# GELU times a gate, streamed through one core: the first tile stored in pieces of two and six rows, the last tile computed in its own input buffer

## The chip, the cores and the metric

The kernel runs on one core of a Trainium2 chip. The metric is the device time of one execution in microseconds (us), the median of several runs. ScalarE (ACT in the profile) computes the GELU, VectorE (DVE) the product, and SyncE (SP) and ScalarE issue DMA transfers. Each of the two issuing engines has a DMA queue of its own; both queues are served by the same 16 DMA engines. TensorE does nothing here.

## The reference

The input x has the shape (32, 512, 2048) in float32. Each row of 2048 is cut into two halves, and the output is the GELU of the first half times the second half:

```
half_dim = x.shape[-1] // 2
x1, x2 = (x[..., :half_dim].copy(), x[..., half_dim:].copy())
gelu_x1 = 0.5 * x1 * (1 + erf(x1 / np.sqrt(2)))
return (gelu_x1 * x2).astype(np.float32)
```

That is 134.2 MB read and 67.1 MB written, and three operations or so for each output element.

## The kernel before

The 16384 rows are cut into 16 tiles of 1024 rows. In a tile every one of the 128 partitions holds R = 8 consecutive rows, so a load of a tile is 8.39 MB, 64 KB in one piece for each partition, and a store is 4.19 MB, 32 KB in one piece for each partition. There are two input buffers (`x_bufs`, each 8 x 2048 floats per partition) and two output buffers (`o_bufs`, each 8 x 1024 floats). Tile i uses the buffers k = i % 2.

The program writes its order and its semaphores by hand. What counts is the order on each engine's own stream:

- SyncE issues the loads (`load`, L48 to L51). Before the loop it issues tile 0 in two halves (rows 0-3 and rows 4-7, here called loads 0a and 0b) and then load 1. In the loop, after tile i's products, it waits for all of them (L114) and issues load i+2 into the buffer that tile i has just given up (L115). At the end it also issues the stores of the last two tiles: store 14 (L110) and the two halves of tile 15, here called stores 15a and 15b (L105).
- ScalarE computes the GELU in steps of rows (L86 to L92): rows 0-1, 2-3 and 4-7 for the first and the last tile, rows 0-4 and 5-7 for the others. It writes the GELU into the output buffer. It also issues the stores of tiles 0 to 13 (L107 and L112), each after waiting for the products it stores (`store`, L53 to L57). Since ScalarE works its stream in order, it can't begin the next GELU while it waits to issue a store. Tile 0 is stored in two halves: rows 0-3 (store 0a) after the products of rows 2-3, and rows 4-7 (store 0b) after the last.
- VectorE multiplies each step in the output buffer by the second halves of the rows (L93 to L102), after waiting for that step's GELU.

Before a tile's first GELU ScalarE waits on one semaphore for its buffer, `ready[k]` (L85; tile 0 waits on `first` instead, L83). Load i counts on it, and so does the store of tile i-2, which has to be out of the output buffer before it is written again. Thus tile i waits for both, and tile 15 for load 15 and store 13. Stores 14, 15a and 15b count on another semaphore, `tail_stored`, which SyncE waits for at the very end (L125).

Of the kernel before, what the change touches and what calls it, by code (L numbers as in the profile page):

```python
# [1 line left out]

# [4 lines left out]

GELU = mybir.ActivationFunctionType.Gelu


@with_exitstack
def kernel(
    ctx: ExitStack,
    tc: tile.TileContext,
    x: bass.AP,
    out: bass.AP,
):
    nc = tc.nc
    P = nc.NUM_PARTITIONS

    x_flat = x.flatten_outer_dims()
    out_flat = out.flatten_outer_dims()
    n_rows, dim = x_flat.shape
    half = dim // 2

    R = 8
    x_t = x_flat.rearrange("(n p r) d -> n p r d", p=P, r=R)
    o_t = out_flat.rearrange("(n p r) d -> n p r d", p=P, r=R)
    n_tiles = x_t.shape[0]
    x_bufs = [nc.alloc_sbuf_tensor(f"x{k}_tile", [P, R, dim], x.dtype) for k in range(2)]  # L30
    o_bufs = [nc.alloc_sbuf_tensor(f"o{k}_tile", [P, R, half], out.dtype) for k in range(2)]

    first = [nc.alloc_semaphore(f"first{j}") for j in range(2)]
    ready = [nc.alloc_semaphore(f"ready{k}") for k in range(2)]
    gelu_done = nc.alloc_semaphore("gelu_done")
    mul_done = nc.alloc_semaphore("mul_done")
    tail_stored = nc.alloc_semaphore("tail_stored")
    opened = nc.alloc_semaphore("opened")  # L40
    scrap = nc.alloc_sbuf_tensor("scrap_tile", [8, 128], x.dtype)
    n = {sem.name: 0 for sem in [*first, *ready, gelu_done, mul_done, tail_stored, opened]}

    def counted(ins, sem, by):
        ins.then_inc(sem, by)
        n[sem.name] += by

    def load(i, rows, sem):  # L48
        ins = nc.sync.dma_start(out=x_bufs[i % 2][:, rows, :], in_=x_t[i][:, rows, :])  # L49
        counted(ins, sem, 16)  # L50
        return ins  # L51

    def store(queue, i, rows, sem):  # L53
        queue.wait_ge(mul_done, n[mul_done.name])
        counted(
            queue.dma_start(out=o_t[i][:, rows, :], in_=o_bufs[i % 2][:, rows, :]), sem, 16
        )  # L57

    opening = nc.scalar.dma_start(out=scrap[:, :], in_=x_t[0][:8, 0, :128])
    counted(opening, opened, 16)
    for ins in (
        opening,
        load(0, slice(0, 4), first[0]),
        load(0, slice(4, 8), first[1]),
        load(1, slice(0, 8), ready[1]),
    ):  # L70
        tc.no_tile_sem_insts.add(ins.ins.name)
    tc.close()
    tc.compile()  # L73

    for i in range(n_tiles):
        k = i % 2
        last = i == n_tiles - 1
        pieces = i == 0 or last
        steps = ((0, 2), (2, 4), (4, 8)) if pieces else ((0, 5), (5, 8))
        for lo, hi in steps:  # L80
            rows = slice(lo, hi)
            if i == 0 and lo % 4 == 0:
                nc.scalar.wait_ge(first[lo // 4], 16)  # L83
            elif lo == 0:
                nc.scalar.wait_ge(ready[k], n[ready[k].name])  # L85
            counted(  # L86
                nc.scalar.activation(  # L87
                    out=o_bufs[k][:, rows, :], in_=x_bufs[k][:, rows, :half], func=GELU
                ),
                gelu_done,  # L90
                1,
            )  # L92
            nc.vector.wait_ge(gelu_done, n[gelu_done.name])  # L93
            counted(
                nc.vector.tensor_mul(  # L95
                    out=o_bufs[k][:, rows, :],
                    in0=o_bufs[k][:, rows, :],
                    in1=x_bufs[k][:, rows, half:],
                ),
                mul_done,  # L100
                1,
            )  # L102
            if pieces and hi % 4 == 0:
                if last:
                    store(nc.sync, i, slice(hi - 4, hi), tail_stored)  # L105
                else:
                    store(nc.scalar, i, slice(hi - 4, hi), ready[k])  # L107
        if not pieces:
            if i == n_tiles - 2:
                store(nc.sync, i, slice(0, R), tail_stored)  # L110
            else:
                store(nc.scalar, i, slice(0, R), ready[k])  # L112
        if i + 2 < n_tiles:
            nc.sync.wait_ge(mul_done, n[mul_done.name])  # L114
            load(i + 2, slice(0, R), ready[k])  # L115


    nc.scalar.wait_ge(opened, 16)
    nc.scalar.drain()  # L119
    for sem in (*first, *ready, opened):  # L120
        nc.scalar.sem_clear(sem)
    nc.vector.drain()
    nc.vector.sem_clear(gelu_done)
    nc.sync.sem_clear(mul_done)
    nc.sync.wait_ge(tail_stored, n[tail_stored.name]).then_inc(  # L125
        tail_stored, -n[tail_stored.name]
    )


# [1 line left out]
_INS = ['x']  # L131
_OUTS = [((32, 512, 1024), 'float32')]


# [23 lines left out]
```

## Time and profile before

| what | value |
|---|---|
| device time, median of 3 runs | 469.3 us (469.29 to 469.43) |
| profiled execution: span from the first to the last instruction (the page gives no other time of it) | 467.8 us |
| VectorE busy | 140.5 us, 34 products |
| ScalarE busy | 115.5 us, 34 GELUs and one table load |
| DMA | 201.34 MB, 430 GB/s in the mean |
| one tile of 8 rows in the steady stretch | 29.0 us |
| median from issue to landing: whole load, whole store by ScalarE | 44.4 us, 44.7 us |

The span is cut into 40 slices in the page, and a row of digits gives the busy tenths of each engine in each slice; the DMA row is the mean over the 16 DMA engines. The chain of waits goes back from the last instruction through whatever released each step. A wait for several things at once is put down to the one that came last. The trace also has a record of every DMA packet with its queue, size, start and duration, and of every semaphore update.

### The profile page before, as it was taken

The numbers are of one execution on the slowest core, as the hardware profiler recorded it, in microseconds if no ns is written. First come the engines' busy times: TensorE is split into PE (matmuls) and PEld (weight loads), VectorE is DVE, ScalarE is ACT, GpSimd is POOL, SyncE is SP. The second block draws the span as 40 slices with busy tenths as digits, with TensorE's granted clock in tenths as the row PEclk, the third lists the DMA queues.
The fourth block names the chain that finished last, engine by engine and source line by source line (L and its number), as shares of the span: only waits on it lengthen the run. The fifth ranks groups of instructions, "written<-read, shape, count | busy, mean of one in ns | idle before, by whom it ended". The sixth has DMA issues, their size and how long they took to land.

```text
span 467.8 us, 154 instructions
## 1 busy us (share of the span) xinstructions
DVE 140.5 (30%) x34; ACT 115.5 (25%) x35; POOL 0.2 (0%) x4
## 2 busy tenths in 40 slices
DVE  0330515207051060511606115060150702507043
ACT  1320606041060410604105050050501506014060
POOL 0000000000000000000000000000000000000000
DMA  8999999999999999999999999999999999999988
GB/s 359 448 448 448 398 406 496 403 403 448 459 437 403 440 412 493 403 403 448 487 409 403 445 406 493 403 403 448 493 403 403 448 426 471 403 426 426 493 384 379
DMA packets 5057, 201.34 MB, mean 430 GB/s; under 512 B 568, under 2 KB 576, under 8 KB 576
## 3 DMA queue, kind: packets, MB, share of 16 engines
q1 hardware_dynamic: 2880, 142.61, 70.6%
q10 hardware_dynamic: 2176, 58.73, 29.1%
q14 instruction: 1, 0.01, 0.0%
HBM read 134.22 MB, written 67.11 MB: 430 GB/s over the span
## 4 chain that ended last, share of the span: by engine, by line
DMA 76%; DVE 14%; ACT 8%; ACTq 0%; SPq 0%; issue 0%
DMA out_dram<-o_tile 66%; DVE o_tile L95 14%; DMA x_tile<-in_x_dram 10%; ACT o_tile L87 8%; ACTq L119 0%; SPq L49 0%
## 5 line engine op out<-in xcount | busy, mean ns | idle before, releaser
L95 DVE TENSOR_TENSOR o_tile<-o_tile,x_tile 128x5120 f32<-128x5120 f32 (+3 forms) x34 | 140.5, 4171 | 319.7 <-ACT o_tile L87 319.7
L87 ACT ACTIVATE o_tile<-x_tile 128x5120 f32<-128x5120 f32 (+3 forms) x34 | 114.3, 3407 | 337.3 <-DMA out_dram<-o_tile 301.8
L87 ACT ACT_TABLE_LOAD x1 | 1.3, 1283 | 2.9 <-PEq L73 2.9
L142 POOL MEMSET const-bfloat16-1.0<- 128x1 bf16 x1 | 0.1, 102 | 0.0
L142 POOL MEMSET const-uint8-127<- 128x1 uint8 x1 | 0.1, 101 | 0.0
L142 POOL MEMSET const-float32-0.0<- 128x1 f32 x1 | 0.1, 99 | 0.2 <-issue 0.2
L142 POOL MEMSET const-float32-1.0<- 128x1 f32 x1 | 0.1, 98 | 0.0
## 6 DMA issues: line engine op xcount, KB each, us to landing
out_dram<-o_tile ACTq DMA_DIRECT2D x13, 4096.0 KB, 44.7
x_tile<-in_x_dram SPq DMA_DIRECT2D x2, 4096.0 KB, 16.7
out_dram<-o_tile ACTq DMA_DIRECT2D x2, 2048.0 KB, 34.4
out_dram<-o_tile SPq DMA_DIRECT2D x1, 4096.0 KB, 25.2
out_dram<-o_tile SPq DMA_DIRECT2D x2, 2048.0 KB, 7.8
x_tile<-in_x_dram SPq DMA_DIRECT2D x15, 44.4
scrap_tile<-in_x_dram ACTq DMA_DIRECT2D x1, 4.0 KB
```

The source lines that it names most:

```text
L87: nc.scalar.activation(out=o_bufs[k][:, rows, :], in_=x_bufs[k][:, rows, :half], func=GELU),
L95: nc.vector.tensor_mul(out=o_bufs[k][:, rows, :], in0=o_bufs[k][:, rows, :], in1=x_bufs[k][:, rows, half:],),
L142: nc = _bacc.Bacc("TRN2", target_bir_lowering=False, num_devices=1)
```

## The change

Two things change. First, tile 0 is stored as rows 0-1 (2048 floats, 8 KB per partition, 1.05 MB in all) and rows 2-7 (24 KB per partition, 3.15 MB). The store of rows 0-1 stands at the same place in ScalarE's stream as store 0a did, after the GELU of rows 2-3, but waits only for the product of rows 0-1. The store of rows 2-7 stands where store 0b did and waits for all products of the tile.

Second, tile 15 no longer uses an output buffer. Its GELU is written over the first halves of its rows in the input buffer, and the product is written packed into the front of the same buffer: the product of rows r takes the place of 1024 floats from 1024 r on, which lies over input that has been used by then. VectorE therefore also waits for its own earlier product before each product of this tile. Stores 15a and 15b read from the packed place. Tile 15 needs nothing of output buffer 1, so store 13 counts on `tail_stored` instead of `ready[1]`, and tile 15 waits for load 15 alone.

The number of instructions on each engine, the number of DMA transfers, and the order of all other steps stay as they were.

```diff
-    def store(queue, i, rows, sem):
-        queue.wait_ge(mul_done, n[mul_done.name])
-        counted(
-            queue.dma_start(out=o_t[i][:, rows, :], in_=o_bufs[i % 2][:, rows, :]), sem, 16
-        )
+    def store(queue, i, rows, from_, sem, after):
+        queue.wait_ge(mul_done, after)
+        counted(queue.dma_start(out=o_t[i][:, rows, :], in_=from_[:, rows, :]), sem, 16)
...
+    packed = x_bufs[(n_tiles - 1) % 2][:, :, :].rearrange("p r d -> p (r d)")
+    packed = packed[:, : R * half].rearrange("p (r d) -> p r d", d=half)
     for i in range(n_tiles):
         k = i % 2
+        x_buf = x_bufs[k]
         last = i == n_tiles - 1
+        made = packed if last else o_bufs[k][:, :, :]
...
+            gelu = x_buf[:, rows, :half] if last else made[:, rows, :]
             counted(
-                nc.scalar.activation(
-                    out=o_bufs[k][:, rows, :], in_=x_bufs[k][:, rows, :half], func=GELU
-                ),
+                nc.scalar.activation(out=gelu, in_=x_buf[:, rows, :half], func=GELU),
                 gelu_done,
                 1,
             )
+            if last:
+                nc.vector.wait_ge(mul_done, n[mul_done.name])
             nc.vector.wait_ge(gelu_done, n[gelu_done.name])
             counted(
                 nc.vector.tensor_mul(
-                    out=o_bufs[k][:, rows, :],
-                    in0=o_bufs[k][:, rows, :],
-                    in1=x_bufs[k][:, rows, half:],
+                    out=made[:, rows, :], in0=gelu, in1=x_buf[:, rows, half:]
                 ),
                 mul_done,
                 1,
             )
-            if pieces and hi % 4 == 0:
-                if last:
-                    store(nc.sync, i, slice(hi - 4, hi), tail_stored)
-                else:
-                    store(nc.scalar, i, slice(hi - 4, hi), ready[k])
+            done = n[mul_done.name]
+            if last and hi % 4 == 0:
+                store(nc.sync, i, slice(hi - 4, hi), made, tail_stored, done)
+            elif i == 0 and hi == 4:
+                store(nc.scalar, i, slice(0, 2), made, ready[k], done - 1)
+            elif i == 0 and hi == 8:
+                store(nc.scalar, i, slice(2, 8), made, ready[k], done)
         if not pieces:
-            if i == n_tiles - 2:
-                store(nc.sync, i, slice(0, R), tail_stored)
-            else:
-                store(nc.scalar, i, slice(0, R), ready[k])
+            queue = nc.sync if i == n_tiles - 2 else nc.scalar
+            sem = ready[k] if i < n_tiles - 3 else tail_stored
+            store(queue, i, slice(0, R), made, sem, done)
```

## The prediction

> **What bounds the kernel now.** I read the slices of the page first, to see whether anything has idle time; then the groups by shape and the chain of waits, to see what the engines wait for; then the DMA issues and the DMA records of the trace, to see in what order the transfers go; and last the order of instructions at both ends, where a change of stores can act.
>
> The page, its span, its slices and its bytes:
>
> ```profile
> span 467.8 us, 154 instructions
> ...
> DVE  0330515207051060511606115060150702507043
> ACT  1320606041060410604105050050501506014060
> ...
> DMA  8999999999999999999999999999999999999988
> ...
> HBM read 134.22 MB, written 67.11 MB: 430 GB/s over the span
> ```
>
> ScalarE and VectorE idle two thirds of the time; the DMA engines are at nine tenths or more in every slice but the first and the last two, and those are where both parts of the change act. So the question is how much of these edges is really idle. Stretches of the span (columns: length, busy time of each engine, granted clock, DMA share, rate):
>
> ```profile
> 71.40:100.40 29.00, 8.76 (x2) 7.12 (x2) 0.00 (x0) 1.00 1.00 434
> 100.40:448.50 348.10, 105.13 (x24) 85.47 (x24) 0.00 (x0) 1.00 1.00 432
> 448.50:457.60 9.10, 6.34 (x3) 7.21 (x3) 0.00 (x0) 1.00 1.00 432
> 457.60:467.40 9.80, 2.58 (x1) 0.00 (x0) 0.00 (x0) 1.00 0.94 402
> 467.40:467.80 0.40, 0.00 (x0) 0.00 (x0) 0.00 (x0) 1.00 0.00 0
> ```
>
> One tile (8.39 MB in, 4.19 MB out) takes 29.0 us at 434 GB/s, and the tail goes at that rate until the last half microsecond. The DMA records say it more sharply: a 64 KB packet takes 2.418 us, a 32 KB one 1.213, a 16 KB one 0.611 (and one 8 KB packet of the instruction queue 0.309), whether read or written. Each of the 16 DMA engines has 120 packets of 64 KB, 128 of 32 KB and 32 of 16 KB: 290.2 + 155.3 + 19.6 = 465.0 us. The first packet starts at 1.74 and the last ends at 467.37, which is 465.6 us. What is not plain moving is 0.6 us of slow first packets at 1.7 to 4, and about 0.4 us of packets that run over their usual time between 21 and 47 (neighbouring packets overlap a little, so the terms exceed the whole by 0.4). Gaps between packets are under 0.1 us each. The kernel is as long as its bytes.
>
> The chain of waits (start, length, what), its end:
>
> ```profile
> 403.75 44.74 DMA out_dram<-o_tile
> 448.49 0.02 issue
> 448.51 1.91 ACT o_tile L87
> 450.42 1.80 ACTq L119
> 452.22 3.52 ACT o_tile L87
> 455.73 0.02 issue
> 455.76 4.42 DVE o_tile L95
> ```
>
> This seems to name the change's target: the last tile (15) begins when store 13 lands, 44.74 us after its issue. But the issues of the x tile, and the waits, say what is beside it:
>
> ```profile
> DMA to landing us min/median/max: 12.0/44.4/45.4
> ...
> ACT o_tile L87 <- DMA out_dram<-o_tile: 301.8, 14, 21.9
> ACT o_tile L87 <- DMA x_tile<-in_x_dram: 35.6, 3, 20.9
> ```
>
> Load 15, issued at 403.74, takes 44.4, so it lands at about 448.1. In the DMA records the two queues take turns packet by packet (a 64 KB load packet, then a 32 KB store packet), 8 packets of each on every engine, so store 13 and load 15 end within one packet, and the 32 semaphore updates of both arrive between 447.88 and 448.49. The wait on the store is 0.1 to 0.4 us longer than that on the load.
>
> **Part 1, the last tile in its own buffer.** Removed: tile 15's wait for store 13, at most 448.49 - 447.88 = 0.6, by the medians 0.35 us. Is it on the path that sets the end? SyncE issues stores 14, 15a and 15b:
>
> ```profile
> 432.76 27.78 SPq L56 DMA_DIRECT2D out_dram<-o_tile  x3
> 448.51 7.21 ACT L87 ACTIVATE o_tile<-x_tile 128x2048 f32<-128x2048 f32 x3 [21.91 <-DMA out_dram<-o_tile]
> 450.45 4.49 DVE L95 TENSOR_TENSOR o_tile<-o_tile,x_tile 128x2048 f32<-128x2048 f32 x2 [17.71 <-ACT o_tile L87]
> 455.76 4.42 DVE L95 TENSOR_TENSOR o_tile<-o_tile,x_tile 128x4096 f32<-128x4096 f32 x1 [0.81 <-ACT o_tile L87]
> ```
>
> Store 14 was issued at 432.76 but stands behind load 15 on the same queue. By the DMA records its packets run from 447.51 to 457.2-457.6, store 15a from there to 462.06-462.5, and store 15b to 466.9-467.4, with no gap. Store 15a is issued at 455.0, some 2.2 us before the engines need it; 15b at 460.2, 1.85 us before. A first load at the start needs 1.0 us from issue (0.73) to its first packet (1.74), so tile 15 has about 1.2 and 0.85 us to spare. An earlier start only lengthens these. Worth: 0.
>
> Added: two VectorE waits on VectorE's own earlier products. The two products of 2048 that now run in 4.49 us are 2.288 each, so they overlap by 0.09; with the wait the second loses this and about 0.02 for the release (the "issue" rows of the chain): 0.1 us on store 15a, which has 1.2 to spare. The second wait, before the product of 4096, is already satisfied (products of rows 2-3 end at 454.94, it starts at 455.76). Nothing but stores 15a and 15b waits for VectorE there. For this wait VectorE: DVE Perf Modes (The DRAIN you can't avoid) of the Trainium skill says that chained copies with a semaphore after each took as long as without; by it this 0.1 would be 0, and as the sum takes it as hidden, the time is the same by both.
>
> Changed: the GELU writes 2x1024 and 4x1024 with a stride inside the x tile, and the product writes packed into the x tile with both inputs strided. No row of before shows a strided output. Before, one input of the product and the GELU's input were strided already. From below the cost is nothing (the element count is the same, a gain is excluded since no work is left out). From above I take the fixed part doubled: by the rows 2048 -> 2.288 and 4096 -> 4.424 VectorE has 0.15 us fixed; by 1.901 and 3.608 ScalarE has 0.19; along GELU, GELU, GELU, product to store 15b that is 0.73 us, still under 0.85. I take 0, since the strided input shows no price; without the cover it would be +0.73. The stores of tile 15 read 16 KB in one piece per partition as before.
>
> **Part 2, tile 0.** Its product of rows 0-1 ends at 14.73 + 2.29 = 17.02, and ScalarE is free at 12.79 + 3.71 = 16.50, so store 0a goes out at 17.04 instead of 19.26, with 8 KB packets; rows 2-3 wait for rows 4-7 and go in 24 KB packets. Moved bytes are equal, and the packets of one pair take 0.309 + about 0.912 (halfway between 16 and 32 KB) = 1.22 against 2 x 0.611 = 1.22 us: 0. ScalarE is not held longer: its wait is shorter by 2.2 us and the GELU of rows 4-7 waits for load 0b anyway.
>
> Next: load 0b runs until 22.1. Before, store 0a's first packet ran at 24.4, after load 1's first. Two microseconds earlier it gets one or two turns before load 0b's end, 0.31 us each: rows 4-7 land 0.3 to 0.6 us later, and so do store 0b and load 2 (issued at 30.5 and 30.6, now about 31). Load 1 fills the DMA until 45 or more, so both are covered by 14 us; without that cover they would cost the 0.6. Then stores run n = 1 or 2 packets ahead of where they ran: load 1 shares its time with 8 packets of 0.31 and n of 0.91 instead of 8 of 0.61, so it lands at 47.0 - 2.4 + 0.9n = 45.5 (n = 1) or 46.4. Load 2 then takes in n packets of store 1 and lands 1.2n later than 71.4, and so do all later ones; store i-2 lands before load i. In every later period store i is issued 13.3 us after load i lands (tile 1: 47.02 to 60.31), long before store i-1 runs out, and even without a store the load alone fills the engines: load 0b alone moved 4.19 MB in 9.7 us, 433 GB/s. Before tile 15 all bytes of loads and of stores to 13 have gone by, so load 15's last packet still ends at 447.5. Worth: 0.
>
> Unknown: the 0.4 us of stretched packets at 21 to 47, of which 0.25 lies in load 1's first packet, where the store queue joins. It could vanish (-0.4) or double with the earlier joining (+0.4). I take it unchanged, since a joining stays.
>
> **Sum.** 467.8 + 0 + 0 = 467.8 of span. The page gives no time of the profiled execution but its span; the median of the timed runs, 469.3, is 1.5 us above it, and what lies around the span (launch, clearing of semaphores) is not touched. Forecast: 469.3.
>
> **The rivals.**
>
> Slower, at the tail: the in-place forms cost more than my bound, so store 15b comes late and the DMA engines run dry at 462. It decides from 0.85 us more on the way from the start of tile 15 to the issue of 15b, and shows as slower from 1.8. If the product of 4096 took twice its 4.42: +4.4 - 0.85 = +3.6, 472.9. For it: no strided output in the trace. Against: strided inputs already run at 1.04 ns per element. Chance 0.04.
>
> Slower, at the start: each 8 KB store packet stretches the load packet beside it as load 1's first was (0.25): 8 x 0.25 = 2.0, less the 0.25 paid today: 471.1. Against: 16 KB packets did so once of eight. Chance 0.03.
>
> Faster: the chain is right, and the end follows the start of tile 15. By the landings this gives 0.35, 469.0, and only from 0.94 would it show; store 13 would have to land that much after load 15. Against: store 14 fills the DMA until 457.2 anyway. Chance 0.02 for over 0.94.
>
> The memory, not the DMA engines, sets the rate, so the new order of reads and writes changes it. Rows: reads alone 433, mixed 434, writes alone 432 GB/s. If mixing cost as much as the 430 to 434 difference of whole span and steady stretch, 0.9%, over one tile's 29 us, it is 0.3 us either way: 469.0 to 469.6. Chance 0.03 that it goes beyond 0.94, shared 0.01 and 0.02. DMA: Bandwidth & Descriptors (Where 436 GB/s comes from) of the Trainium skill says that for HBM transfers the HBM limit of about 358 GB/s binds; by it, as an estimate, 201.3 MB would take 562 us, and the trace with 430 GB/s does not agree.
>
> **How the numbers follow.** Timed runs of before lie within 0.14 us, but I take 0.2% (0.94 us) as what this kernel can tell from no change. Forecast 0.88, the rivals 0.04, 0.03, 0.02 and 0.03. Slower: 0.04 + 0.03 + 0.02 = 0.09; faster: 0.02 + 0.01 = 0.03; same 0.88. The range takes the stretched packets both ways (469.3 - 0.4 and + 0.4) and 0.1 more above for a tail that uses up its cover: 468.9 to 469.8.
>
> **What would show it.** Store 0a issued near 17.0; tile 1 starting at about 45.5 instead of 47.02; the tiles after it starting 1 to 2.5 us later than before; most of ScalarE's 301.8 us of waiting put down to loads instead of stores; tile 15 starting at 448.1 to 448.5; the last three stores landing without a gap at about 457.9, 462.9 and 467.8. I am wrong if the DMA share drops below 0.9 between 457 and 467, if load packets beside 8 KB packets grow, or if a stretch in the middle falls under 434.

## The result and the profile after

The changed kernel takes 469.86 us (median of 21 runs, 469.59 to 470.25), the kernel before 469.31 (median of 21). The ratio is 1.0012 with a 95% interval of 1.0006 to 1.0017: 0.55 us slower. The forecast was 469.3, with a range that ended at 469.8.

The page of the changed kernel, its span, its slices and its bytes:

```profile
span 468.6 us, 157 instructions
...
DVE  0330512407034070330704307042070520705143
ACT  1330606014060230602306032060320604106060
...
DMA  8999999999999999999999999999999999999998
...
HBM read 134.22 MB, written 67.11 MB: 430 GB/s over the span
```

The span is 0.8 us longer (468.62 against 467.84), the bytes are the same, and the DMA engines are still busy in every slice. The three instructions more (154 before) are VectorE's waits on its own products. Stretches of the changed kernel (columns as before: length, busy time of each engine, granted clock, DMA share, rate):

```profile
71.40:100.40 29.00, 8.76 (x2) 7.12 (x2) 0.00 (x0) 1.00 1.00 434
103.40:451.00 347.60, 105.19 (x25) 87.52 (x26) 0.00 (x0) 1.00 1.00 434
```

So nothing was lost in the steady stretch: 29.0 us for a tile's bytes at 434 GB/s, as before. The end, in order of time:

```profile
435.67 0.35 SPq L55 DMA_DIRECT2D out_dram<-o_tile  x1
448.91 7.22 ACT L90 ACTIVATE x_tile<-x_tile 128x2048 f32<-128x2048 f32 x3 [19.41 <-DMA x_tile<-in_x_dram]
450.93 4.62 DVE L98 TENSOR_TENSOR x_tile<-x_tile 128x2048 f32<-128x2048 f32 x2 [15.29 <-ACT x_tile L90]
455.58 5.44 SPq L55 DMA_DIRECT2D out_dram<-x_tile  x2
456.23 4.42 DVE L98 TENSOR_TENSOR x_tile<-x_tile 128x4096 f32<-128x4096 f32 x1 [0.68 <-ACT x_tile L90]
```

Tile 15 now waits for its load alone, and still starts 0.4 us later than before (448.91 against 448.51). Its GELUs take 7.22 us (7.21 before) and the last product the same 4.42. The tail did what it did before, some tenths later. And the beginning:

```profile
17.03 0.38 ACTq L55 DMA_DIRECT2D out_dram<-o_tile  x1
23.66 3.62 ACT L90 ACTIVATE o_tile<-x_tile 128x4096 f32<-128x4096 f32 x1 [7.18 <-DMA x_tile<-in_x_dram]
27.31 4.43 DVE L98 TENSOR_TENSOR o_tile<-o_tile,x_tile 128x4096 f32<-128x4096 f32 x1 [8.10 <-ACT o_tile L90]
31.76 0.36 ACTq L55 DMA_DIRECT2D out_dram<-o_tile  x1
47.13 7.12 ACT L90 ACTIVATE o_tile<-x_tile 128x5120 f32<-128x5120 f32 x2 [19.86 <-DMA x_tile<-in_x_dram]
```

Store 0a goes out at 17.03, 2.2 us earlier, as the change says. But the second half of tile 0 lands 1.2 us later (its GELU starts at 23.66, not 22.47), and tile 1 starts at 47.13 where 45.5 to 46.4 was forecast.

The records of the DMA packets show the loss itself. A record doesn't name its DMA engine, but each packet starts within a few ns of the end of another, and followed in this way the records fall into 16 chains, one for each engine. Below are the packets of one chain in both kernels: start in us, L for a load and S for a store, size in KB, and after a plus the ns over the usual time of that size (8 KB 309, 16 KB 611, 24 KB 912, 32 KB 1213, 64 KB 2418).

```
before: 20.5:L32 21.7:L64+381 24.5:S16 25.1:L64 27.5:S16 28.1:L64 30.5:S16 ... 43.3:L64 45.7:S16 46.3:L64 48.7:S16
after:  18.2:L32 19.4:L32+552 21.2:S8 21.5:L32 22.7:S8 23.0:S8 23.3:L64 25.8:S8 ... 36.6:S8 36.9:L64 39.4:L64+69 41.8:S24 42.8:L64+164 45.3:S24
```

The load packet that is under way when a store begins takes longer. Before, this happens once, when store 0a joins load 1. After, it happens twice: when store 0a joins load 0b, and again around store 0b's first 24 KB packet, in load 1's last two packets. (This is the order in 12 of the 16 chains. In the other four one more load packet goes ahead of the store's first packet both times; the first time the stretched packet is the one ahead of that load packet, the second time it is that load packet itself.) Summed over all packets that took longer than usual between 10 and 70 us and divided by 16 engines, it is 0.41 us before and 1.03 after. The difference, 0.62, accounts for the 0.55 us of the medians and for most of the 0.78 by which the last packet ends later (468.15 against 467.37); in the mean over the 16 chains the last packet ends 0.64 later. After 70 us the sum is 0.03 in either kernel.

### The profile page after: what moved, and what is told of

Read it like the earlier page. It is cut to its first block, busy times and chain, and to the rows that moved or that the text cites. A ratio compares the mean times of both kernels' runs of the same rounds, so it can differ in the third digit from the quotient of the medians.

```text
span 468.6 us, 157 instructions
## 1 busy us (share of the span) xinstructions
DVE 140.6 (30%) x34; ACT 115.5 (25%) x35; POOL 0.2 (0%) x4
## 4 chain that ended last, share of the span: by engine, by line
DMA 76%; DVE 14%; ACT 8%; ACTq 0%; SPq 0%; issue 0%; DVEq 0%
DMA out_dram<-o_tile 57%; DMA x_tile<-in_x_dram 19%; DVE o_tile L98 13%; ACT o_tile L90 7%; ACT x_tile L90 1%; DVE x_tile L98 1%; ACTq L121 0%; SPq L49 0%; DVEq L96 0%
## 5 line engine op out<-in xcount | busy, mean ns | idle before, releaser
L98 DVE TENSOR_TENSOR o_tile<-o_tile,x_tile 128x5120 f32<-128x5120 f32 (+3 forms) x31 | 131.6, 4284 | 304.1 <-ACT o_tile L90 304.1
L90 ACT ACTIVATE o_tile<-x_tile 128x5120 f32<-128x5120 f32 (+3 forms) x31 | 107.0, 3498 | 318.3 <-DMA out_dram<-o_tile 282.7
L98 DVE TENSOR_TENSOR x_tile<-x_tile 128x2048 f32<-128x2048 f32 (+1 forms) x3 | 9.0, 3004 | 16.0 <-ACT x_tile L90 16.0
L90 ACT ACTIVATE x_tile<-x_tile 128x2048 f32<-128x2048 f32 (+1 forms) x3 | 7.2, 2467 | 19.4 <-DMA x_tile<-in_x_dram 19.4
## 6 DMA issues: line engine op xcount, KB each, us to landing
out_dram<-o_tile ACTq DMA_DIRECT2D x13, 4096.0 KB, 44.7
x_tile<-in_x_dram SPq DMA_DIRECT2D x15, 39.7
```

The source lines that it names most:

```text
L90: nc.scalar.activation(out=gelu, in_=x_buf[:, rows, :half], func=GELU),
L98: nc.vector.tensor_mul(out=made[:, rows, :], in0=gelu, in1=x_buf[:, rows, half:]),
```

## The experiments

Every run that is compared by a ratio was timed against the kernel before on the same chip. "Stretched" below is the sum just described, per DMA engine.

### One part alone

The tail part alone, twice (the second time together with later runs):

```diff
-            elif i == 0 and hi == 4:
-                store(nc.scalar, i, slice(0, 2), made, ready[k], done - 1)
-            elif i == 0 and hi == 8:
-                store(nc.scalar, i, slice(2, 8), made, ready[k], done)
+            elif i == 0 and hi % 4 == 0:
+                store(nc.scalar, i, slice(hi - 4, hi), made, ready[k], done)
```

> Tile 0 is stored as before (rows 0-3, rows 4-7); tile 15 is computed in its own buffer as in the change. Theory A (the 0.55 us come from load packets that are stretched while tile 0's stores join the DMA engines; the tail is hidden behind stores 14 and 15a): within 0.15 us of before, 469.3, span 467.8, and stretched packets of about 0.4 us per DMA engine between 15 and 50 us as before. Theory B (the strided forms or the added waits of tile 15 delay the last store): about 469.9, with a gap in front of store 15b's packets.

> The tail part alone once more, beside the two others on one chip: 469.15 to 469.4, as before, with 0.4 to 0.5 us of stretched packets between 15 and 65 us and store 15b behind 15a without a gap.

Measured: 469.26 us, ratio 0.9999 (0.9990 to 1.0007), and 469.19, ratio 0.9999 (0.9990 to 1.0008). Stretched: 0.50 and 0.48 us. The end of the first of them:

```profile
448.51 7.22 ACT L90 ACTIVATE x_tile<-x_tile 128x2048 f32<-128x2048 f32 x3 [21.70 <-DMA x_tile<-in_x_dram]
450.53 4.62 DVE L98 TENSOR_TENSOR x_tile<-x_tile 128x2048 f32<-128x2048 f32 x2 [17.58 <-ACT x_tile L90]
455.18 5.44 SPq L55 DMA_DIRECT2D out_dram<-x_tile  x2
```

The wait for store 13 is gone (the releaser is now the load). It was worth 0.18 us: in both profiles that is how much later the last of store 13's semaphore updates comes than the last of load 15's (448.67 and 448.49 in the first, 448.46 and 448.28 in the second). In the first profile load 15 was itself late by as much, so that tile 15 starts at 448.51 as it did with the wait; in the second it starts at 448.31, 0.2 us earlier, and the time is the same as before all the same. The two products that wait for one another take 4.62 instead of 4.49 us. Theory B is out.

The head part alone (tile 15 keeps its output buffer and its wait for store 13):

```diff
-        made = packed if last else o_bufs[k][:, :, :]
+        made = o_bufs[k][:, :, :]
...
-            gelu = x_buf[:, rows, :half] if last else made[:, rows, :]
+            gelu = made[:, rows, :]
...
-            if last:
-                nc.vector.wait_ge(mul_done, n[mul_done.name])
...
-            sem = ready[k] if i < n_tiles - 3 else tail_stored
+            sem = ready[k] if i < n_tiles - 2 else tail_stored
```

> Tile 0 is stored as rows 0-1 early and rows 2-7; tile 15 uses its output buffer and waits for store 13 as before. Theory A: all of the change's loss, about 469.85, with 1.0 us of stretched packets per DMA engine between 15 and 50 us, half at the first packet of store 0a and half around the first of store 0b. Theory B: about 469.3.

Measured: 470.0 us, ratio 1.0016 (1.0007 to 1.0025), stretched 1.03 us: 0.41 before 25 us and 0.61 between 38 and 50. The whole loss belongs to the head part.

The changed kernel once more:

> The changed kernel once more, for its profile: whether the stretches of 0.5 us at 19 to 21 us and at 39 to 46 us come back at the same places (they belong to the order of transfers) or elsewhere (chance).

Measured: 469.78 us (one run), stretched 0.52 at 19 to 22 us and 0.44 at 39 to 46 us, where it was 0.51 and 0.52. The stretches come back at the same places: they belong to the order of the transfers.

### Issue time or size

The changed sizes at the old time:

```diff
-                store(nc.scalar, i, slice(0, 2), made, ready[k], done - 1)
+                store(nc.scalar, i, slice(0, 2), made, ready[k], done)
```

> As the change, but store 0a (rows 0-1) waits for the product of rows 2-3 too, so it is issued at 19.26 us as before, with 8 KB packets. Within theory A two causes are told apart. A1 (when the stores join matters: the first joining while load 0b still runs, and store 0b beginning in the middle of load 1): store 0a starts at about 24.4 and store 0b at the end of load 1, so 469.3 to 469.45 and 0.3 to 0.5 us of stretched packets. A2 (the sizes matter: 8 KB or 24 KB packets): 469.7 to 469.9 as the change, with 0.5 us of stretched packets around store 0b's first.

Measured: 469.38 us, ratio 1.0002 (0.9993 to 1.0011). Stretched 0.52 us: 0.03 where store 0a joins, 0.18 between 25 and 38 (0.12 there in the kernel before), 0.29 in load 2's first packet. Its store 0a and its tile 1:

```profile
19.38 0.38 ACTq L55 DMA_DIRECT2D out_dram<-o_tile  x1
44.50 7.12 ACT L90 ACTIVATE o_tile<-x_tile 128x5120 f32<-128x5120 f32 x2 [18.25 <-DMA x_tile<-in_x_dram]
```

With nothing changed but the issue time of store 0a, which is some 2.2 us later, the loss is gone within what can be measured: the eleven runs took 469.24 to 469.66, the eleven of the head part alone, timed with them on the same chip, 469.73 to 470.47. Store 0a's joining costs 0.03 beside load 1's 64 KB packets; the same 8 KB packets cost 0.5 beside load 0b's 32 KB ones. The size by itself is not free: store 0b now begins at the border of loads 1 and 2, as it does before, and the first packet of load 2 is stretched by 0.29 ahead of the first 24 KB packet, where in the kernel before nothing is stretched ahead of the first 16 KB packet.

Rows 0-2 and 3-7:

```diff
-                store(nc.scalar, i, slice(0, 2), made, ready[k], done - 1)
+                store(nc.scalar, i, slice(0, 3), made, ready[k], done)
...
-                store(nc.scalar, i, slice(2, 8), made, ready[k], done)
+                store(nc.scalar, i, slice(3, 8), made, ready[k], done)
```

> Store 0a is rows 0-2 (12 KB packets), issued at 19.3 us, store 0b rows 3-7 (20 KB). If the issue time is what counts, as the runs with rows 0-1 late suggest, 469.2 to 469.4 with 0.3 to 0.5 us of stretched packets between 15 and 65 us: a joining of 0.03 to 0.25 (between the 8 KB and the 16 KB store's) and at most 0.3 at the end of load 1. If a piece that is no power of two costs by itself, both 12 KB and 20 KB do and the time is 469.6 or more.

Measured: 469.26 us, ratio 0.9999 (0.9990 to 1.0008), stretched 0.61 us (0.15 at the joining, 0.30 between 38 and 50, most of it in load 2's first packet). A piece that is no power of two costs nothing by itself. The 0.2 us of stretch more than before don't show in the time; other packets, those of the first microseconds above all (0.45 to 0.65 us from one profile to the next), vary by as much.

Three stores, the first as early as in the change:

```diff
-            elif i == 0 and hi == 4:
-                store(nc.scalar, i, slice(0, 2), made, ready[k], done - 1)
-            elif i == 0 and hi == 8:
-                store(nc.scalar, i, slice(2, 8), made, ready[k], done)
+            elif i == 0:
+                if hi == 2:
+                    early = done
+                elif hi == 4:
+                    store(nc.scalar, i, slice(0, 2), made, ready[k], early)
+                    store(nc.scalar, i, slice(2, 4), made, ready[k], done)
+                else:
+                    store(nc.scalar, i, slice(4, 8), made, ready[k], done)
```

> As the change, but tile 0 goes out in three stores: rows 0-1 as early as in the change, rows 2-3 at 19.3 us, rows 4-7 as before. The store queue joins as early as in the change, has no 24 KB packet, and does not run out before load 1 ends. A1: the early joining still costs 0.5 us per DMA engine at 19 to 21 us, the second stretch of 0.5 us near 40 us is gone: 469.4 to 469.6. A2: if 8 KB packets are the cause, 469.8 or more; if 24 KB packets are, both stretches are gone and the time is 469.3.

Measured: 474.33 us, ratio 1.0107 (1.0094 to 1.0121), which no theory had expected. In order of time:

```profile
58.70 0.36 ACTq L55 DMA_DIRECT2D out_dram<-o_tile  x1
88.77 7.12 ACT L90 ACTIVATE o_tile<-x_tile 128x5120 f32<-128x5120 f32 x2 [36.24 <-DMA out_dram<-o_tile]
93.27 8.76 DVE L98 TENSOR_TENSOR o_tile<-o_tile,x_tile 128x5120 f32<-128x5120 f32 x2 [34.60 <-ACT o_tile L90]
102.06 0.36 ACTq L55 DMA_DIRECT2D out_dram<-o_tile  x1
```

Tile 2 starts at 88.77 (71.40 before), because the last store of tile 0 landed only then. The two queues take turns packet by packet whatever a packet's size, and the completion write of a transfer takes a turn too. Three stores are 24 packets and 3 completions on every engine, so they need the turns of loads 1, 2 and nearly all of load 3. Load 4 needs tile 2's buffer and so is issued at 102.06, but load 3's last packet had ended by 91.9 and store 1's by 100.5: all 16 engines then stood idle until 103.0 to 104.5, 2.5 to 4.4 us each, and load 4's first packets were stretched by another 1.2. The joining itself behaved as in the change, 0.34 us before 25 us. So the early joining costs without a 24 KB packet behind it too. Nor is the second stretch the 24 KB packet's alone: where the second store (8 KB packets) and the third (16 KB) begin, the last packets of loads 1 and 2 are stretched by 0.21 and 0.42. What the 24 KB packet adds can't be read from this time.

Tile 0 loaded as rows 0-1 and 2-7, so that store 0a joins still earlier and beside 48 KB packets:

```diff
-        load(0, slice(0, 4), first[0]),
-        load(0, slice(4, 8), first[1]),
+        load(0, slice(0, 2), first[0]),
+        load(0, slice(2, 8), first[1]),
...
-            if i == 0 and lo % 4 == 0:
-                nc.scalar.wait_ge(first[lo // 4], 16)
-            elif lo == 0:
+            if i == 0 and lo < 4:
+                nc.scalar.wait_ge(first[lo // 2], 16)
+            elif i > 0 and lo == 0:
...
-            elif i == 0 and hi == 4:
-                store(nc.scalar, i, slice(0, 2), made, ready[k], done - 1)
+            elif i == 0 and hi == 2:
+                store(nc.scalar, i, slice(0, 2), made, ready[k], done)
```

> As the change, but tile 0 is loaded as rows 0-1 and rows 2-7, so store 0a (8 KB) is issued near 12 us and joins load 0b's 48 KB packets, and its 8 packets are gone when store 0b (24 KB) joins in the middle of load 1. If a joining costs the more the larger the first store packet (8 KB 0.03, 16 KB 0.25 to 0.35, 32 KB 1.1 us beside 64 KB load packets), the first costs under 0.3 and the second 0.5 to 0.9: 469.6 to 470.2. If a joining inside tile 0's load costs 0.5 whatever the packets, 0.5 at 13 to 16 us and more behind it.

Measured: 469.56 us, ratio 1.0007 (0.9998 to 1.0016), stretched 0.43 us before 25 us and 0.42 where store 0b joins an otherwise empty store queue (a load packet at 37 us takes 2.8 instead of 2.42). Neither theory had both numbers: the first joining is dearer than 0.3, the second cheaper than 0.5. Joining inside tile 0's load costs 0.3 to 0.5 in every run that did it.

### Joining later

One store of 8 rows:

```diff
-            elif i == 0 and hi == 4:
-                store(nc.scalar, i, slice(0, 2), made, ready[k], done - 1)
             elif i == 0 and hi == 8:
-                store(nc.scalar, i, slice(2, 8), made, ready[k], done)
+                store(nc.scalar, i, slice(0, 8), made, ready[k], done)
```

> As the change, but tile 0 goes out as one store of 8 rows (32 KB packets) after its last product, issued near 30.6 us, so the store queue joins once, in the middle of load 1. If each joining in the middle of a load stretches load packets by about 0.5 us per DMA engine whatever the size, there is one such stretch at 33 to 40 us and none at 19 to 25: in all 0.5 us, 469.3 to 469.45. If only small or odd packets cause it, nothing is stretched after 15 us and the time is 468.9 to 469.1.

Measured: 470.95 us, ratio 1.0028 (1.0018 to 1.0037), single runs from 469.65 to 471.36; the profile is of a run of 471.36, and the four runs under 470 have none. Neither expectation had it: there is one joining, but with 1.20 us of stretch. With a 32 KB store packet next, load packets at 34 us take 3.3 to 4.5 us instead of 2.42. One DMA engine had two of them and stayed some 2 us behind the others to the end, and that shows in the tail:

```profile
450.60 7.22 ACT L90 ACTIVATE x_tile<-x_tile 128x2048 f32<-128x2048 f32 x3 [18.23 <-DMA x_tile<-in_x_dram]
452.62 4.62 DVE L98 TENSOR_TENSOR x_tile<-x_tile 128x2048 f32<-128x2048 f32 x2 [14.11 <-ACT x_tile L90]
457.27 5.44 SPq L55 DMA_DIRECT2D out_dram<-x_tile  x2
```

Tile 15 starts when the last engine's part of its load is in (450.60). The others had long gone on with store 14 and finished it at 457.7 to 458.3; store 15a, issued at 457.27, came 0.1 to 0.5 us too late for ten of them and store 15b 0.1 to 0.3. Here the cover of the tail, about 1 us, was used up.

Both stores issued behind the GELU of rows 4-7, with the sizes of the change (the edit below) and with those of before (the same, with rows 0-3 and 4-7):

```diff
-            elif i == 0 and hi == 4:
+            elif i == 0 and hi == 8:
                 store(nc.scalar, i, slice(0, 2), made, ready[k], done - 1)
-            elif i == 0 and hi == 8:
                 store(nc.scalar, i, slice(2, 8), made, ready[k], done)
```

> As the change, but store 0a (rows 0-1) stands behind the GELU of rows 4-7 and is issued near 26 us, so it joins in the middle of load 1 with 8 KB packets; store 0b (24 KB packets) follows it in the queue without running dry, in load 2. If the place of joining makes the cost: 0.5 us at 28 to 31 us. If the first packets of the 24 KB store make it: 0.3 to 0.5 us near 50 us. The stores end some packets into load 3, which delays tile 2 by up to 10 us but leaves load 4 time, so beside that 469.4 to 469.9.

> The same with rows 0-3 and rows 4-7, 16 KB packets in both stores. If the place of joining makes the cost: 0.5 us at 28 to 31 us as in the run with 8 KB and 24 KB packets. If the sizes do: less than 0.3 us in all, and 469.2 to 469.3.

Measured: 476.81 us, ratio 1.0171 (1.0153 to 1.0190), and 477.66, ratio 1.0179 (1.0166 to 1.0193). Both expectations were wrong, and on the issue time too: ScalarE's queue issued store 0a at 22.5, as soon as the GELU had begun. The joining costs 0.02 with 8 KB and 0.34 with 16 KB packets. The rest is new. The last packet of load 1 is stretched by 0.22 and 0.55, although no store begins there. And from load 4 on, near 100 us, packets are stretched in every load, by 0.2 to 0.7 us each time, 5.7 and 6.3 us in all after 70 us. (The DMA engines also drift apart: the last one ends 2.7 us after the first in both runs, where it is 0.4 before.) Stretches of one tile's length, in the run with 16 KB packets (a packet counts whole in the stretch in which it starts, so single rows swing; the sums above are from the records):

```profile
100.00:129.00 29.00, 8.76 (x2) 7.12 (x2) 0.00 (x0) 1.00 1.01 434
129.00:158.00 29.00, 8.76 (x2) 7.12 (x2) 0.00 (x0) 1.00 1.01 432
216.00:245.00 29.00, 8.76 (x2) 7.12 (x2) 0.00 (x0) 1.00 1.00 424
245.00:274.00 29.00, 8.76 (x2) 7.12 (x2) 0.00 (x0) 1.00 1.01 426
400.00:429.00 29.00, 8.76 (x2) 7.12 (x2) 0.00 (x0) 1.00 1.02 434
```

Here every store's completion is written 3.6 us after that of the load beside it, one load and one store packet later; before, the two go together (302.5 and 302.5 us, for one), in the change the store's comes 3.6 or 7.3 us ahead, and there the steady stretch stays at 434. So in these two runs most of the loss came with the place in which tile 0's stores left the store queue against the load queue, not with the joining. That the place is the cause is not shown: no run changed it alone.

## Why the prediction was right or wrong

**The tail: right.** It was costed at 0 because stores 14 and 15a cover tile 15. The tail alone measures 0.9999 (twice). The removed wait, taken as 0.35 us by the medians and not on the path, is 0.18, and a start 0.2 us earlier bought nothing. The wait on the products, taken as 0.1 us and hidden, is 0.13 and hidden; the other value that the prediction gives for it, 0, doesn't fit the trace. The strided forms cost 0.01 us on three GELUs and nothing on the last product, where up to 0.73 had been allowed. Of the rivals, the slower tail, the rate set by the memory and the earlier end are out: the steady stretch runs at 434 GB/s as before, and stores 14, 15a and 15b complete 4.9 us apart in both kernels.

**The head: the mechanism right, one term mis-sized.** The step that failed is "Unknown: the 0.4 us of stretched packets at 21 to 47 ... It could vanish (-0.4) or double with the earlier joining (+0.4). I take it unchanged, since a joining stays." Measured, 0.41 became 1.03 and, in the second profile, 0.96. The term was left with a bound instead of a price, and the bound of a doubling was too narrow: a second stretch was not counted. With packets of 8 KB instead of 16 KB the early store is through before load 1 ends, so store 0b's first packet meets load 1's last packets instead of the border between two loads, and there as much is lost (0.52) as at the first (0.51). One of the prediction's signs of being wrong, load packets that grow beside 8 KB packets, was seen at store 0a's first. With +0.62 in place of 0 the sum is 469.9, against 469.86 measured.

**The rival at the start: the right place, the wrong mechanism.** It let each 8 KB packet stretch its neighbour, 2.0 us in all. Beside the 8 KB packets between 25 and 38 us no load packet is stretched at all; it is where a store begins.

**The order of transfers: half right.** Load 0b landed later by 1.2 us, not 0.3 to 0.6: one or two packets of 8 KB, 0.31 us each, went ahead of its last packet and its completion, and the stretch of 0.5 came on top. Tile 1 started at 47.13, not 45.5 to 46.4, and tile 2 at 74.35, 2.95 later than before, not 1.2 to 2.4. In the chains two of the 24 KB packets go ahead of load 1's completion, the prediction's n = 2; with its 46.4 and 2.4 for that and the 0.6 us of added stretch both numbers come out within 0.2. Later tiles stayed there without any loss on the way, as forecast, and tile 15 started 0.4 us later than before (448.91), not at 448.1 to 448.5: that is part of the loss itself.

**The attribution: wrong.** Most of ScalarE's waiting was to move from stores to loads, since stores now land first. The completion writes agree (tile 7 starts at 219.41, 0.02 us after the last of load 7's at 219.39, the last of the store's having come at 214.34), but the waits still name the store:

```profile
ACT o_tile L90 <- DMA out_dram<-o_tile: 282.7, 13, 22.0
ACT o_tile L90 <- DMA x_tile<-in_x_dram: 35.7, 3, 19.9
ACT x_tile L90 <- DMA x_tile<-in_x_dram: 19.4, 1, 19.4
```

Load and store count on one semaphore, and the view can't tell which came last. For tile 15, whose semaphore has only the load left, it names the load. The times from issue to landing suffer in the same way: the page of the changed kernel gives 39.7 us for a load and 44.7 for a store, while by the completion writes load 7 took 44.7 and the store beside it 39.7. On the page of before the 44.4 and 44.7 are those of the pair as well.

**What stays open.** Where the loss arises is shown: by undoing either part, by moving the issue time alone, and by adding up packets. Why a load packet is stretched when a store begins is not. Store size, load packet size, an empty or a continued queue, and the place against the load's border all seem to matter, no two-number rule from these runs gives all of them, and one store of 16 KB packets that began in the middle of load 2 (the second store of the run with 16 KB packets behind the GELU) stretched nothing. None of the versions beats the kernel before by more than can be measured.

## What to carry to other kernels

When the DMA engines never rest, as here, a wait that is removed, or a store that goes out earlier, buys nothing: count bytes and look only for what could make the engines pause. What is left to win or lose is in how the queues meet: where a second queue joins, how large its first packet is, and where its transfers end against those of the other queue. And since turns go by packets and not by bytes, cutting a store into more pieces delays its last piece: one extra piece made a buffer free 17 us later and cost 5 us.

## What the runs showed of the hardware that was not expected

A store queue that begins beside running loads costs time, and in these runs the price grew with the size of the first packet. Beside 64 KB load packets: 0.02 to 0.03 us for 8 KB, 0.15 for 12 KB, 0.21 to 0.34 for 16 KB, 0.42 for 24 KB on an empty queue, 1.2 for 32 KB. An 8 KB packet costs 0.34 to 0.52 beside 32 KB loads and 0.43 beside 48 KB ones. In the steady stretch of before and after, where each 32 KB store follows another, a store's beginning costs nothing. Size isn't all of it, as the two runs with both stores behind the GELU show: a 16 KB store that followed another stretched nothing, and load 1's last packet was stretched where no store began.

The completion write of a transfer takes a turn of its own between the queues. After store 0a's last packet two load packets run back to back (36.9 and 39.4 in the line above) with nothing but store 0a's completion, at 39.4, between them.

In the two runs where the stores ended 3.6 us behind the loads, the loads were stretched anew in every tile from load 4 on, by 0.2 to 0.7 us each.
